# A decoder trunk on one core: start addresses of moving and stationary matmul operands

## Chip, core and metric

The kernel runs on one core of one Trainium2 chip. The metric is the device time of one execution in microseconds: the median of three runs before the change is 1049.02 us (1048.88 to 1049.52).

## What is computed

Two layers over 256 tokens of width 1024, in float32. Each layer is a macaron block: half a SwiGLU feed-forward, a mixer, half a second SwiGLU, and a gated input embedding, each added to the scaled stream and layer-normalised. The mixer is forgetting attention (FoX) in the first layer and multi-head latent attention (MLA) in the second.

```python
def swiglu(x, w_in, w_out):
    h = x @ w_in
    gate, up = h[..., :D_FF], h[..., D_FF:]
    return (jax.nn.silu(gate) * up) @ w_out
...
    for i in range(DEPTH):
        if i == N_A:
            k_nope, k_rope, v_shared = shared_kv(x, kv_w_down, kv_norm, kv_w_up, cos, sin)
        x = post_norm(x, 0.5 * swiglu(x, ffn1_w_in[i], ffn1_w_out[i]), ln_g[i, 0], ln_b[i, 0])
        ...
        x = post_norm(x, mix, ln_g[i, 1], ln_b[i, 1])
        x = post_norm(x, 0.5 * swiglu(x, ffn2_w_in[i], ffn2_w_out[i]), ln_g[i, 2], ln_b[i, 2])
        gate = jax.nn.sigmoid((x @ ple_w_gate[i] + ple_b_gate[i]).astype(jnp.float32)).astype(x.dtype)
        x = post_norm(x, gate * (p[i] @ ple_w_proj[i]), ln_g[i, 3], ln_b[i, 3])
```

D_MODEL is 1024, D_FF 2816, FoX has 16 heads of 64, MLA 16 heads of 128 + 64 (rotary) with a key/value latent of 256 and a query latent of 384.

## The kernel before

Every product is made of three matmuls in TensorE's fast float32 form (`mm3`, L608): each operand is split into a rounded high part and a low remainder, and high·high, high·low and low·high are summed in PSUM. ScalarE writes the high part (`nc.scalar.activation`, L252), VectorE the low part (`tensor_tensor`, L253). `mm(out, lhsT, rhs)` (L615) loads `lhsT` as the **stationary** operand (a LDWEIGHTS of 128 columns, row `PEld` of the profile) and streams `rhs`, the **moving** operand, past it. In a row of the profile, `h<-xT,hl` says that the PSUM bank `h` was written from `xT` and `hl`; it doesn't say which of the two moved.

A stream (`Stream`, L145) brings weights in by DMA in a fixed order, up to three 1 MB groups ahead, and splits them into slots in SBUF: `hl0` to `hl9`, and `gb`, `qk`, `fs`, `ota`, `otb` when these are lent. `place` (L221) makes the tile of a slot: 2112 columns, of which 2048 are used (high part, then low part 4096 bytes further). It starts 48 columns (192 bytes) into the slot for the keys of `moves` (L427): the FoX value weights `fv`, and the gate weights `pg` of layer 0. All other keys start at column 0.

What moves past what, by stage:

- `HT` (L807), most hidden chunks of a feed-forward: weight columns (`wiu`) stationary, the transposed stream `xT` moving, two token tiles of 128 columns in one matmul.
- `H` (L734) through `moving` (L652), two hidden chunks by two token tiles in each of three feed-forwards: `xT` stationary, weights `win` moving, 512 columns.
- `sums` (L859): the hidden activations of a chunk, in seven combinations, stand in one of the four homes `fs`, `qk`, `ota`, `otb` and are stationary; output weights `ws` move, 512 columns. 21 matmuls a chunk.
- FoX: `VA`, `VB`, `VC` (from L1129) with `xT` stationary and `fv` (512 columns), `fvb` (256) and `fvc` (272) moving; the output projection `O` with the attention output in `ota` and `otb` stationary and `fo` moving, 512 columns.
- MLA: `q_rope` with the query latents `cqt` stationary and `qr` moving; `V` with the key/value latents `ckv` stationary and `kvv` moving; `gen` with weights `kvk` and `qn` stationary and `ckv` and `cqt` moving, 256 columns; `QK` with, among others, the rotated queries (in `xT`'s place) stationary and the rotated keys `kr` moving; `O` with the attention output in `otb`, `ota` and `fs` stationary and `mo` moving.
- The input gate `ple` (L1057): `xT` stationary, `pg` moving; 512 columns, and 256 for the last token tile of layer 1.

The order of instructions on each engine is fixed when the program is built: by the lists `FOX` (L49) and `ORDER` (L71) in the mixers, and elsewhere by the stream's own rules, which use estimated times and no addresses. Tiles are laid out in SBUF in the order of their first use. One thing the reader needs beyond the code is where they start; the start address modulo 256 bytes, before:

| tile | start modulo 256 |
|---|---|
| `xT`, `ones` | 160 |
| `fs`, `hl0` to `hl9`, `gb`, `qk`, `g4`, `P` | 224 |
| `ota`, `otb` | 96 |
| `PT` | 160 |
| `ident`, `raw`, `p1` | 128 |

Inside these tiles, operands begin at multiples of 256 bytes from the tile's start, but for the shift of 48 columns, `ckv` (48 columns into `fs`, so 160), and `fvc`, whose blocks of 272 columns begin 1088 bytes apart (64 modulo 256).

Of the kernel before, what the change touches and what calls it, by code (L numbers as in the profile page):

```python
# [10 lines left out]
F32 = mybir.dt.float32  # L11
F32R = mybir.dt.float32r
# [132 lines left out]
class Stream:  # L145
# [74 lines left out]

    def place(self, key, slot):  # L221
        w = self.pool.tile([128, 2112], F32R, tag=slot, name=slot, bufs=1)
        c = 48 if moves(key) else 0
        return w[:, c : c + 2048].rearrange("p (i c) -> p i c", i=2)

    def split(self, half=False):
        self.later()
        nc = self.nc
        key = self.order[self.ready]
        g = group_of(key)  # L230
        while self.sums_left(key):
            self.add(g)
        src, parts, n = unit_of(key, self.raw[g], self.sums.get(g))
        if self.aside(key):
            w = self.pool.tile([128, 2, 512], F32R, tag="g4", name="g4", bufs=6)
        else:
            slot = self.slots.pop(0)
            self.slot_of[key] = slot
            w = self.place(key, slot)
        hi, lo = w[:parts, 0, :n], w[:parts, 1, :n]  # L240
        shape = src.shape
        if len(shape) == 3:
            hi = hi.rearrange("p (a b) -> p a b", b=shape[2])
            lo = lo.rearrange("p (a b) -> p a b", b=shape[2])
        elif len(shape) == 4:
            hi = hi.rearrange("p (a b c) -> p a b c", b=shape[2], c=shape[3])
            lo = lo.rearrange("p (a b c) -> p a b c", b=shape[2], c=shape[3])
        t = self.arrives[group_of(key)]
        self.act_t, self.dve_t = max(self.act_t, t), max(self.dve_t, t)

        def both():
            nc.scalar.activation(hi, src, AF.Copy)  # L252
            nc.vector.tensor_tensor(lo, src, hi.bitcast(F32), op=ALU.subtract)  # L253

        if key[0] == "pb":
            nc.gpsimd.memset(w[:, 0, :].bitcast(F32), 0.0)
            lo = w[32:33, 0, :n]
            both()
        elif half:
            nc.scalar.activation(hi, src, AF.Copy)  # L260
            self.busy(act=n)

            def rest():
                nc.vector.tensor_tensor(lo, src, hi.bitcast(F32), op=ALU.subtract)  # L264
                self.busy(dve=n)
                self.split_done(key, w)

            self.rest = rest
            return
        else:  # L270
            both()
        self.pair(n)
        self.split_done(key, w)

    def aside(self, key):
# [148 lines left out]
    return key  # L424


def moves(key):  # L427
    return key[0] == "fv" or key[:2] == ("pg", 0)


def unit_of(key, raw, sums=None):

    k, u = key[0], key[-1] % 2
    if k in ("win", "fv"):
        return raw.rearrange("p (k c) -> p k c", c=512)[:, 2 * u : 2 * u + 2, :], 128, 1024
    if k == "wiu":
        return raw[:, 1024 * u : 1024 * u + 1024], 128, 1024
    if k == "ws":
        i = key[-1]
        return ((raw, sums)[i // 2])[:, 1024 * u : 1024 * u + (512 if i == 3 else 1024)], 128, 512 if i == 3 else 1024  # L440
    if k == "fvc":
        n = 816 if key[-1] < 2 else 544
        return raw[:, n * u : n * u + n], 128, n
    if k in ("wout", "fvb", "fo", "pg", "pp", "mo", "qr"):
        return raw[:, 1024 * u : 1024 * u + 1024], 128, 1024
    if k in ("fk", "fq"):
        return raw.rearrange("p (k c) -> p k c", c=256)[:, :, 128 * u : 128 * u + 128], 128, 1024
    if k == "pb":
        return raw[0:1, 0:1024], 1, 1024
    if k == "kd":  # L450
        return raw[:, 640 * u : 640 * u + 640], 128, 640
    if k == "dq":
        return raw[:, 768 * u : 768 * u + 768], 128, 768
    if k == "qn":
        return raw[:, 512:1280], 128, 768
    if k == "kvv":
        return raw[:, 0:1024], 128, 1024
    if k == "kvk":
        return raw[:, 0:512], 128, 512
    raise KeyError(key)  # L460
# [50 lines left out]
class Trunk:  # L511
# [24 lines left out]
    def home(self, homes):  # L536

        if self.rec:
            return None, Dummy()
        self.S.retire()  # L540
        tag = next(t for t in homes if t not in self.S.slot_of.values() and t not in self.taken)
        self.taken.add(tag)
        return tag, self.own([128, 2, 896], F32R, tag)

    def dma(self, out, in_):
# [578 lines left out]
    def fox(self, li):  # L1124
        nc, S, a = self.nc, self.S, self.a
# [26 lines left out]
        def VC(t, at={}):  # L1152

            ps = self.bank("y")
            for k in range(8):
                if k in at:
                    at[k]()
                if k % 3 == 0:
                    w = self.use(("fvc", k // 3))
                c = 272 * (k % 3)  # L1160
                self.mm3(
                    ps[:, 0:272], lambda i: self.xT[:, t, i, k, :], lambda i: w[:, i, c : c + 272], k == 0, k == 7)
            if (t, 1) not in v:
                v[t, 1] = self.tl([128, 2, 512], F32R, "g4", 6)
            o = v[t, 1]
            nc.scalar.activation(ftok[:, t, 112:128], ps[:, 256:272], AF.Copy)
            self.parts(o[:, 0, 256:512], o[:, 1, 256:512], ps[:, 0:256])
# [17 lines left out]
        self.tl([128, 8], F32, "gap2", 1)  # L1185
        mb = self.tl([128, 2, 2, 384], F32, "gb", 1)
        cq = self.tl([128, 16, 2], F32, "cq", 1)
        fr = slice(96, 128)
        nc.gpsimd.memset(bf, 0.0)
        if not self.rec:  # L1190
# [3 lines left out]
        f, e, u, r, ab = (fs[fr, 256 * i : 256 * i + 256] for i in range(5))  # L1194
# [224 lines left out]
        def hold(x):  # L1419
# [7 lines left out]
            gb=lambda: self.load_gb(li, 1), ln=lambda t: self.ln(t, y[t], ALPHA, LN_EPS), dl=decay_load, dm=decay_mask,  # L1427
# [47 lines left out]

    def kv_transpose_rope(self):
        nc = self.nc
        self.kr = self.kvt[:, 1088:1856].rearrange("p (i t c) -> p t i c", t=2, i=3)
        kr = [self.kr[:, :, i, :] for i in range(3)]
        b = self.bank("tr")  # L1480
        for t in range(2):
            self.transpose(b[:, 128 * t : 128 * t + 128], self.kvtok[:, t, 256:384])
        nc.gpsimd.memset(kr[1][64:128].bitcast(F32), 0.0)
        nc.gpsimd.memset(kr[2][0:64].bitcast(F32), 0.0)
        b2 = b[:, 0:256].rearrange("p (t c) -> p t c", t=2)
        nc.scalar.activation(kr[0], b2, AF.Copy)
        for s in range(2):
            r = slice(64 * s, 64 * s + 64)
            nc.vector.tensor_tensor(kr[1 + s][r], b2[r], kr[0][r].bitcast(F32), op=ALU.subtract)
# [12 lines left out]
    def mla(self, li):  # L1502
# [3 lines left out]
            self.dma(qn, pbcast(a["mla_q_norm"][0], QR))  # L1506
        scale = float(192 ** -0.5)
        v = {}
        cqt = self.tl([128, 2, 2, 3, 128], F32R, "gb", 1)
        cqtok = self.tl([128, 2, 768], F32, "PT", 1)  # L1510
        S.reclaim("otb", "qk")
        home = {}
# [422 lines left out]
```

## Time and profile before

| | |
|---|---|
| median of three runs | 1049.02 us |
| the profiled execution | 1049.6 us |
| its span | 1047.8 us |
| matmuls | 7085 |
| VectorE busy | 891.8 us |
| ScalarE busy | 592.9 us |
| HBM | 202.74 MB moved by DMA, mean 193 GB/s |

The granted clock is full in all 40 slices of the span. The profile's times are from one execution; all offsets in the rows are counted from its span's start. A matmul's end is modelled and overlaps the next one's start, so of matmuls the starts are to be read, and the distance between them.

### The profile page before, as it was taken

What the parts mean: (1) busy time and instruction counts of PE and PEld (TensorE: products, weight loads), DVE (VectorE), ACT (ScalarE), POOL (GpSimd) and SP (SyncE); (2) the same over time, 40 slices, a digit from 0 to 9 for tenths busy, and PEclk for the clock granted to TensorE, in tenths of its full rate; (3) what the DMA queues carried; (4) which work ended last, traced back from release to release, by engine and by line L of the source; (5) the groups of instructions that cost most, each with busy time, mean ns of one, the idle gap of its engine ahead of it and who ended that gap; (6) DMA issues with size and microseconds to landing.
All of it is one profiled execution on the core that took longest, in us unless ns stands there. A gap on an engine that the chain in (4) does not pass through costs nothing.

```text
span 1047.8 us, 17555 instructions
## 1 busy us (share of the span) xinstructions
PE 1035.6 (99%) x7085; PEld 948.6 (91%) x7085; DVE 891.8 (85%) x1312; ACT 592.9 (57%) x901; POOL 58.0 (6%) x88
## 2 busy tenths in 40 slices
PE   9999999999999999999999999999999999999996
PEld 8999898899889999998899898988999889898986
DVE  5788977868898979978979899888887989889877
ACT  6555563666755555663565646646776564646541
POOL 0000000122300000000220000000000000000000
PEclk9999999999999999999999999999999999999999
DMA  7855586455636363673674545743445564555732
GB/s 281 305 191 188 185 298 243 162 168 169 216 128 246 121 252 125 241 282 132 236 260 151 195 169 190 270 142 112 145 156 179 183 214 162 200 190 176 271 125 81
DMA packets 37476, 202.74 MB, mean 193 GB/s; under 512 B 3970, under 2 KB 9874, under 8 KB 16532
## 3 DMA queue, kind: packets, MB, share of 16 engines
q1 hardware_dynamic: 37396, 201.63, 54.3%
q8 instruction: 55, 0.90, 0.3%
q14 instruction: 25, 0.20, 0.1%
HBM read 200.55 MB, written 1.06 MB: 192 GB/s over the span
## 4 chain that ended last, share of the span: by engine, by line
PE 95%; DVE 2%; ACT 1%; issue 1%; DMA 0%; SPq 0%; DVEq 0%; ACTq 0%
PE h L616 53%; PE y L616 29%; PE tr L616 10%; PE tr L620 2%; DVE hl L253 1%; PE h L620 1%; DMA raw<-in_w_dram 0%; PE tr L1375 0%; DVE ts L300 0%; DVE x L705 0%; DVE tr L1720 0%; ACT qk L629 0%; DVE PT L633 0%; DVE ts L306 0%; DVE raw L308 0%
## 5 line engine op out<-in xcount | busy, mean ns | idle before, releaser
L616 PE MATMUL h<-xT,hl 128*128 128x256 f32 x3144 | 366.1, 277 | 1.2 <-ACT hl L327 0.7
L616 PEld LDWEIGHTS h<-xT,hl 128*128 128x128 f32 x3144 | 362.0, 188 | 2.9 <-ACT hl L327 1.2
L253 DVE TENSOR_TENSOR hl<-raw,hl 128x1024 fp32r<-128x1024 f32 (+5 forms) x271 | 314.2, 1190 | 36.1 <-ACT hl L252 35.0
L252 ACT ACTIVATE hl<-raw 128x1024 fp32r<-128x1024 f32 (+5 forms) x271 | 267.8, 1027 | 70.6 <-DVE raw L308 41.3
L616 PE MATMUL y<-hl,g 128*128 128x512 f32 x336 | 78.6, 391 | 0.0
L616 PEld LDWEIGHTS y<-hl,g 128*128 128x128 f32 x336 | 62.5, 188 | 12.6
L616 PE MATMUL h<-hl,xT 128*128 128x512 f32 (+2 forms) x312 | 67.9, 371 | 0.0
L616 PEld LDWEIGHTS h<-hl,xT 128*128 128x128 f32 x312 | 54.9, 188 | 9.8
L616 PE MATMUL y<-hl,otb 128*128 128x512 f32 x219 | 58.0, 399 | 0.0
L264 DVE TENSOR_TENSOR hl<-raw,hl 128x1024 fp32r<-128x1024 f32 (+2 forms) x44 | 52.3, 1192 | 0.8 <-ACT hl L260 0.7
L616 PE MATMUL y<-hl,xT 128*128 128x512 f32 (+3 forms) x282 | 52.7, 334 | 0.0
L260 ACT ACTIVATE hl<-raw 128x1024 fp32r<-128x1024 f32 (+2 forms) x44 | 45.2, 1029 | 9.7 <-DVE raw L308 9.1
L629 ACT ACTIVATE xT<-tr 128x512 fp32r<-128x512 f32 x28 | 16.1, 597 | 58.9 <-PE tr L620 58.9
L616 PEld LDWEIGHTS y<-hl,xT 128*128 128x128 f32 x282 | 44.1, 188 | 4.6 <-ACT xT L629 0.4
L616 PEld LDWEIGHTS y<-hl,otb 128*128 128x128 f32 x219 | 39.8, 188 | 8.4 <-DVE otb L633 0.3
L616 PE MATMUL y<-hl,ota 128*128 128x512 f32 x177 | 46.8, 398 | 0.1
L700 POOL TENSOR_TENSOR rs<-ve,mhalf 128x1 f32<-128x1 f32 x16 | 15.1, 942 | 519.8 <-DVE ve L699 519.8
L616 PE MATMUL tr<-xT,hl 128*128 128x256 f32 x360 | 42.5, 277 | 0.0
L616 PEld LDWEIGHTS tr<-xT,hl 128*128 128x128 f32 x360 | 41.7, 188 | 0.4
L616 PEld LDWEIGHTS y<-hl,ota 128*128 128x128 f32 x177 | 32.7, 189 | 7.7 <-DVE hl L253 0.6
L823 ACT ACTIVATE P<-h 128x512 f32<-128x512 f32 x33 | 19.7, 596 | 33.0 <-PE h L616 32.6
L300 DVE TENSOR_TENSOR ts<-raw 128x1024 f32<-128x1024 f32 x29 | 35.4, 1222 | 0.6
(322 smaller groups left out, 1632.7 us busy)
## 6 DMA issues: line engine op xcount, KB each, us to landing
raw<-in_ffn_in_dram SPq DMA_DIRECT2D x85, 1024.0 KB, 5.0
raw<-in_ffn_out_dram SPq DMA_DIRECT2D x44, 1024.0 KB, 5.0
raw<-in_pg_dram SPq DMA_DIRECT2D x8, 1024.0 KB, 4.9
raw<-in_mo_dram SPq DMA_DIRECT2D x8, 1024.0 KB, 4.8
raw<-in_kq_dram SPq DMA_DIRECT2D x8, 640.0 KB, 4.2
gb<-in_ln_g_dram SPq DMA_DIRECT2D x8, 512.0 KB, 5.9
gb<-in_ln_b_dram SPq DMA_DIRECT2D x8, 512.0 KB, 7.5
raw<-in_fk_dram SPq DMA_DIRECT2D x4, 1024.0 KB, 5.6
```

The costliest lines, as they stand in the source:

```text
L252: nc.scalar.activation(hi, src, AF.Copy)
L253: nc.vector.tensor_tensor(lo, src, hi.bitcast(F32), op=ALU.subtract)
L260: nc.scalar.activation(hi, src, AF.Copy)
L264: nc.vector.tensor_tensor(lo, src, hi.bitcast(F32), op=ALU.subtract)
L300: tt(s[:, 0:1024].rearrange("p (a b) -> p a b", b=512), r[:, 0:512][:, None, :].to_broadcast([128, 2, 512]), r[:, 512:1536].rearrange("p ( ...
L616: self.nc.tensor.matmul(out, lhsT, rhs, start=start, stop=stop)
L620: self.nc.tensor.transpose(out, in_, self.ident)
L629: self.nc.scalar.activation(hi, src, AF.Copy)
L700: nc.gpsimd.tensor_tensor(rs, ve, self.mhalf, op=ALU.pow)
L823: nc.scalar.activation(gt, ps, AF.Silu)
```

## The change

No instruction is added, removed or moved on any engine, and no DMA changes. Two unused tiles of 128 bytes, `gap4` and `gap5`, are laid out ahead of `ota` and behind the small tiles of FoX: `ota`, `otb` and the statistics tiles behind them begin 128 bytes later than before (`ota` and `otb` so at 224 modulo 256), and all that follows `gap5`, `PT`, `nrm`, `p1` and `raw` among it, 256 bytes later (the same modulo 256). `place` now shifts more keys: by 48 columns (192 bytes) the feed-forward weights `win` that move, `kvv` and `qr`; by 32 columns (128 bytes) `fvb` and `fvc`. The blocks of `fvc` are set 320 columns apart instead of 272, so that their splits write three (or two) pieces of 272 columns instead of one of 816 (or 544). The latents `cqt` lie 192 bytes into their tile, and the rotated keys `kr` 128 bytes further in than before. Modulo 256, moving operands then start as follows:

| moving operand | before | after | stationary operand |
|---|---|---|---|
| `win`, `kvv`, `qr` in `hl`, `qk`, `fs`, `gb` | 224 | 160 | `xT`, `ckv` 160; `cqt` 224, then 160 |
| the same and `fv`, `pg` of layer 0 in `ota`, `otb` | 96, 32 | 160 | 160 |
| `fvb` | 224 | 96 | `xT` 160 |
| `fvc` | 224, 32, 96 | 96 | `xT` 160 |
| `cqt` | 224 | 160 | `qn` 224 |
| `kr` | 224 | 96 | rotated queries 160 |
| `ws`, `fo`, `mo` | 224 | 224 | in `ota`, `otb`: 96, then 224 |
| `xT` | 160 | 160 | weights in `ota`, `otb`: 96, then 224 |

```diff
     def place(self, key, slot):
         w = self.pool.tile([128, 2112], F32R, tag=slot, name=slot, bufs=1)
-        c = 48 if moves(key) else 0
+        c = shift(key)
         return w[:, c : c + 2048].rearrange("p (i c) -> p i c", i=2)
...
         if len(shape) == 3:
-            hi = hi.rearrange("p (a b) -> p a b", b=shape[2])
-            lo = lo.rearrange("p (a b) -> p a b", b=shape[2])
+            b = n // shape[1]
+            hi = hi.rearrange("p (a b) -> p a b", b=b)[:, :, 0 : shape[2]]
+            lo = lo.rearrange("p (a b) -> p a b", b=b)[:, :, 0 : shape[2]]
...
-        self.pair(n)
+        self.pair(math.prod(shape[1:]))
...
-def moves(key):
-    return key[0] == "fv" or key[:2] == ("pg", 0)
+def shift(key):
+
+    if key[0] in ("fv", "kvv", "qr") or key[:2] == ("pg", 0) or key[0] == "win" and key[1:3] != (0, "ffn1"):
+        return 48
+    return {"fvb": 32, "fvc": 32}.get(key[0], 0)
...
     if k == "fvc":
         n = 816 if key[-1] < 2 else 544
-        return raw[:, n * u : n * u + n], 128, n
+        return raw[:, n * u : n * u + n].rearrange("p (a b) -> p a b", b=272), 128, n // 272 * 320
...
         self.taken.add(tag)
+        if tag == "ota":
+            self.tl([128, 32], F32, "gap4", 1)
         return tag, self.own([128, 2, 896], F32R, tag)
...
-                c = 272 * (k % 3)
+                c = 320 * (k % 3)
...
         cq = self.tl([128, 16, 2], F32, "cq", 1)
+        self.tl([128, 32], F32, "gap5", 1)
...
-        self.kr = self.kvt[:, 1088:1856].rearrange("p (i t c) -> p t i c", t=2, i=3)
+        self.kr = self.kvt[:, 1120:1888].rearrange("p (i t c) -> p t i c", t=2, i=3)
...
-        cqt = self.tl([128, 2, 2, 3, 128], F32R, "gb", 1)
+        cqt = self.tl([128, 1584], F32R, "gb", 1)[:, 48:1584].rearrange("p (t i k c) -> p t i k c", t=2, i=2, k=3)
```

## The prediction

> **What bounds the kernel now.** I read the page first, for the engine that sets the end, and then the matmul rows of the timeline, because this change alters nothing but addresses.
>
> ```profile
> PE 1035.6 (99%) x7085; PEld 948.6 (91%) x7085; DVE 891.8 (85%) x1312; ACT 592.9 (57%) x901; POOL 58.0 (6%) x88
> PE 95%; DVE 2%; ACT 1%; issue 1%; DMA 0%; SPq 0%; DVEq 0%; ACTq 0%
> ```
>
> TensorE is busy 99% of the span and carries 95% of the chain that ended last. So a nanosecond off the spacing of matmuls is nearly a nanosecond off the end, unless a wait on another engine takes it back.
>
> The busy time of a row is modelled, so I use the **spacing** instead: the start of the next row minus the start of this one, over the count. Here are three chunks of a `sums` stage, 21 matmuls of 512 columns each (6+3+3+3+3+3), alike but for the home tile of the stationary operand: first `qk`, then `ota`, then `otb`.
>
> ```profile
> 629.26 1.52 PE L616 MATMUL y<-hl,qk 128*128 128x512 f32 x6
> ...
> 634.02 1.56 PE L616 MATMUL y<-hl,ota 128*128 128x512 f32 x6
> ...
> 638.90 1.56 PE L616 MATMUL y<-hl,otb 128*128 128x512 f32 x6
> ...
> 643.78 0.87 PE L616 MATMUL h<-xT,hl 128*128 128x256 f32 x6
> ```
>
> On `qk` the chunk takes 634.02 − 629.26 = 4.76 us, 226.7 ns a matmul. On `ota` and on `otb` it takes 4.88 us, 232.4 ns. By the table of start addresses, the moving operand stands at 224 (modulo 256 bytes) in all three; the stationary one at 224 in `qk` and at 96 in the other two. I call moving minus stationary, modulo 256, the **offset**: 0 against 128. The same operation on the same data sizes costs 5.7 ns more at offset 128.
>
> **The change part by part.** Nothing is removed or added in work: every engine has the same instructions in the same order, and DMAs are the same in size and number. Only three splits of the `fvc` weights write three (or two) separate runs of 272 columns instead of one run. What changes is the offset of some matmuls.
>
> *Sums on `ota` and `otb`, offset 128 to 0.* How many there are comes from these groups:
>
> ```profile
> L616 PE MATMUL y<-hl,otb 128*128 128x512 f32 x219 | 58.0, 399 | 0.0
> L616 PE MATMUL y<-hl,ota 128*128 128x512 f32 x177 | 46.8, 398 | 0.1
> L616 PE MATMUL y<-gb,otb 128*128 128x512 f32 x21 | 5.7, 394 | 0.0
> L616 PE MATMUL y<-gb,ota 128*128 128x512 f32 x3 | 0.9, 393 | 0.0
> L616 PE MATMUL h<-hl,ota 128*128 128x512 f32 x21 | 6.1, 398 | 0.0
> L616 PE MATMUL h<-hl,otb 128*128 128x512 f32 x15 | 4.3, 398 | 0.0
> L616 PE MATMUL h<-gb,otb 128*128 128x512 f32 x3 | 0.9, 398 | 0.0
> ```
>
> A chunk writes `h` three times and `y` twelve times. The `h` rows hold 21 + 15 + 3 = 39, so there are 13 chunks; at 0.12 us each that is 1.56 us. It is not all kept. In one stage VectorE has no slack:
>
> ```profile
> 404.00:440.00 36.00, 36.00 (x232) 32.31 (x231) 35.20 (x43) 22.92 (x27) 0.00 (x0) 1.00 0.51 175
> ```
>
> VectorE is busy 35.20 of 36.00 us there, so TensorE's two chunks in that stage (0.24 us) end in a longer wait for VectorE. I count 11 chunks: **1.32 us**. The bounds are 0 (the offset is not the cause) and 1.56.
>
> *Output projections with the stationary attention output in `ota` or `otb`, offset 128 to 0.* The four `y` rows hold 420 matmuls; without 13 × 12 of the sums, 264 remain. They come in long runs and in sixes:
>
> ```profile
> 286.75 3.11 PE L616 MATMUL y<-hl,otb 128*128 128x512 f32 x12
> 289.70 2.96 PE L616 MATMUL y<-hl,ota 128*128 128x512 f32 x12
> 292.50 2.96 PE L616 MATMUL y<-hl,otb 128*128 128x512 f32 x12
> ...
> 752.06 1.56 PE L616 MATMUL y<-hl,otb 128*128 128x512 f32 x6
> 753.45 1.53 PE L616 MATMUL tr<-hl,fs 128*128 128x512 f32 x6
> ...
> 819.59 4.40 PE L616 MATMUL y<-hl,fs 128*128 128x512 f32 x18
> 823.82 5.75 PE L616 MATMUL y<-hl,ota 128*128 128x512 f32 x24
> 829.40 0.60 PE L620 MATMUL tr<-ident,x 128*128 128x128 f32 x4
> ```
>
> Twelve at offset 128 take 292.50 − 289.70 = 2.80 us, 233.3 ns each; six take 1.39 us, 231.7. The last two heads have their output in `fs` (224, offset 0), and that row speaks for caution: 4.23 us for 18 is 235.0, no better than the 232.5 of the 24 on `ota` behind it. Seen from inside, the run settles:
>
> ```profile
> 822.23 1.76 PE L616 MATMUL y<-hl,fs 128*128 128x512 f32 x7
> ```
>
> The last seven take 823.82 − 822.23 = 1.59 us, 227.1 ns, so the eleven before them took 240 each, start-up included. So offset 0 has to be entered: the first half dozen after a change of work stay slow, and then the spacing locks near 227. For runs of 24 and more (48 in the first mixer, 24 at the end of the second) I take 5 ns on 72: 0.36 us. For the 192 in short runs I take 231.7 − 230 = 1.7 ns, 230 being midway between a settled 227 and the 233.3: 0.33 us. Together **0.7 us**, bounds 0 and 264 × 5.7 ns = 1.5.
>
> *The latents `cqt` moving past `qn` weights, offset 0 to −64, 256 columns.* Here the best offset is another one:
>
> ```profile
> 592.42 24.06 PE L616 MATMUL h<-xT,hl 128*128 128x256 f32 x210
> 616.32 2.88 PE L616 MATMUL h<-xT,gb 128*128 128x256 f32 x24
> ...
> 726.90 1.22 PE L616 MATMUL h<-gb,hl 128*128 128x256 f32 x9
> 727.96 0.49 PE L620 MATMUL tr<-ident,P 128*128 128x128 f32 x3
> ...
> L616 PE MATMUL h<-gb,hl 128*128 128x256 f32 x144 | 19.6, 281 | 0.0
> ```
>
> `xT` (160) past weights at 224, offset −64, takes 23.90 us for 210, 113.8 ns; the latents at offset 0 take 1.06 us for nine, 117.8. Moving them to 160 makes them the first case: 144 × 4.0 ns = **0.58 us**, bounds 0 and 0.65.
>
> *Weights `win` moving past `xT`, offset 64 to 0, 512 columns.* The kernel holds its own comparison. The gate of the per-layer input already shifts its weights in layer 0 and not in layer 1. The same 36 matmuls:
>
> ```profile
> 497.13 2.88 PE L616 MATMUL y<-hl,xT 128*128 128x512 f32 x12
> ...
> 505.34 1.03 PE L620 MATMUL tr<-ident,x 128*128 128x128 f32 x8
> ...
> 1015.85 2.91 PE L616 MATMUL y<-hl,xT 128*128 128x512 f32 x12
> ...
> 1024.11 1.03 PE L620 MATMUL tr<-ident,x 128*128 128x128 f32 x8
> ```
>
> Shifted they take 8.21 us (228.1 ns), unshifted 8.26 (229.4): 1.4 ns. Three feed-forward blocks run four hidden tiles of 24, so 288 × 1.4 ns = **0.4 us**. The upper bound is 288 × (229.4 − 226.7) = 0.8. The lower one is a small loss, since offset 0 is entered slowly. In the second `fv` run, also shifted, 24 take 5.51 us (229.6): 0.1 us lost.
>
> ```profile
> 204.61 1.55 PE L616 MATMUL y<-otb,xT 128*128 128x512 f32 x6
> ...
> 210.12 2.05 PE L616 MATMUL h<-xT,hl 128*128 128x256 f32 x16
> ```
>
> The first six of that run lie in a slot of `otb` and stand at offset 128 even with the shift (`win` there, without it, at −64). There are some 50 such matmuls, weights that landed in `ota` or `otb` and move past `xT`:
>
> ```profile
> L616 PE MATMUL y<-otb,xT 128*128 128x512 f32 x24 | 6.2, 394 | 0.0
> L616 PE MATMUL h<-otb,xT 128*128 128x512 f32 x18 | 4.8, 393 | 0.0
> L616 PE MATMUL h<-ota,xT 128*128 128x512 f32 x12 | 3.4, 401 | 0.0
> ```
>
> All but the second gate's six become like the rest: 48 × 3 ns (an estimate, 232.4 to 229.4), **0.15 us**.
>
> *Weights `fvb` and `fvc` past `xT`, offset 64 (and mixed) to −64, 48 matmuls each.*
>
> ```profile
> 195.48 2.99 PE L616 MATMUL h<-hl,xT 128*128 128x256 f32 x24
> 198.31 3.54 PE L616 MATMUL y<-hl,xT 128*128 128x272 f32 x27
> 201.69 0.60 PE L620 MATMUL tr<-ident,fs 128*128 128x128 f32 x2
> ```
>
> `fvb` takes 2.83 us for 24, 117.9 ns, and goes to the offset at which `xT` runs at 113.8: 0.2 us. `fvc` takes 3.38 us for 27, about 126; with the same 4 ns, 0.2 us, from which I keep half because no run of 272 columns at one offset stands in the trace. **0.3 us**, bounds 0 and 0.4.
>
> *The rest.* `kvv` (48, in sixes) and `kr` (48, in ones and twos) are in runs too short to settle; the `qr` products keep offset 0, as both operands move by 192. I take 0, with ±0.1 us as bounds. Matmuls that read `xT` past weights in `ota` or `otb` go from offset 64 to −64 and stay at the 113.8 of the row above.
>
> The sum is 1.32 + 0.7 + 0.58 + 0.4 + 0.15 + 0.3 = 3.45 us. In the second mixer some of it ends in waits, since scores, softmax and transposes alternate between engines; I take off 0.15. That leaves **3.3 us**. The profiled execution took 1049.6 us (span 1047.8), 0.6 above the median of the runs, and a gain of matmul spacing is the same in each. So the median goes from 1049.0 to **1045.7 us**.
>
> One rule of the notes speaks against all of it. The Trainium skill, "TensorE: Matmul & The Clock Gate", section "Step-by-step: what each phase is for", gives TensorE two independent read ports into SBUF, so that loading the next weights takes nothing from the matmul that runs. By it an offset between the two addresses could not matter and the time would stay 1049.0. The trace differs: 226.7 against 232.4 ns in neighbouring chunks.
>
> **The rivals.** *No price in the address.* The spacing hangs on something that goes with the home tile by chance (its place in the chunk order, say), and all shifts do nothing: 1049.0. For it: `qk` always comes before `ota`. Against it: the gate's 36 matmuls, which differ in layer and shift alone. This is the case that the rule above describes.
>
> *Only long runs gain.* Locking needs ten or more matmuls at one offset. Then sums, latents and the 72 long-run projections count, and the entry of each `win` and `fv` run eats the rest; with waits 1.3 + 0.36 + 0.3 = 2.0 us: 1047.0.
>
> *Everything locks.* Because neighbours now share an offset, runs enter settled: 1.56 + 1.5 + 0.65 + 0.8 + 0.15 + 0.4 = 5.1 us: 1043.9. For it: the chunk on `qk` above entered settled from `fs`.
>
> *The wide majority unlocks (slower).* The 256-column products of `xT` run at 113.8 because they are settled; unsettled, such a product costs the 117.8 of the latents. Weights in `ota` and `otb` reach offset −64 from 64, and a run that enters unsettled could stay so into the rows behind. Each costs 4.0 ns, and the page's largest row has 3144. If all fall it is 12.6 us against 3.3 gained: 1058.3. The point from which the kernel is slower by 0.2% is (3.3 + 2.1) / 4.0 ns, some 1,350 matmuls. Against it: 210 in a row at −64 average 113.8, with transposes just ahead of them.
>
> **How the numbers follow.** Forecast 0.57, everything locks 0.20, only long runs 0.13, no price 0.07, majority unlocks 0.03. The likeliest gives 1045.7. The range runs from 1043.7, just beyond full locking, to 1047.6, just beyond long runs alone. About 0.2% (2.1 us, to 1046.9) is what a measurement of this kernel tells from no change. Faster by more: nearly all of the first two cases and some of the third, 0.79. Within it: 0.18. Slower: 0.03.
>
> **What would show it.** In the changed kernel's timeline, chunks of sums on `ota` and `otb` should take 4.76 us like those on `qk`; the latents' nines about 1.02 us; the first `fvb` run of 24 about 2.73; the long projection run 227 ns once settled; and the wait for VectorE near 429 us should be longer. It is wrong if the `ota` chunks stay at 4.88, or if rows of `xT` past `hl` leave 113.8.

## The result and the profile after

| | before | after |
|---|---|---|
| median in the same rounds (8 runs each) | 1049.27 us (1048.68 to 1050.36) | 1046.36 us (1044.89 to 1048.34) |
| the profiled execution | 1049.6 us | 1046.09 us |
| its span | 1047.8 us | 1044.3 us |

The ratio of the medians is 0.9972, with a 95% interval from 0.9962 to 0.9983: faster by 1.8 to 4.0 us. In five further rounds the same kernel had 1045.69 us beside 1048.97, a ratio of 0.9969 (0.9957 to 0.998).

On the page of the changed kernel the engines' line and the chain of waits read as follows.

```profile
PE 1032.6 (99%) x7085; PEld 948.6 (91%) x7085; DVE 892.0 (85%) x1312; ACT 593.3 (57%) x901; POOL 58.8 (6%) x88
PE 91%; DVE 5%; ACT 1%; issue 1%; DMA 0%; SPq 0%; DVEq 0%; ACTq 0%
```

TensorE still sets the end, and its matmuls are 3.0 us shorter; VectorE's share of the chain has grown from 2 to 5%, since a faster TensorE reaches a few waits sooner. Line 616 is now line 622.

The three chunks of a sums stage, in the timeline of the changed kernel (start, modelled length, engine, line, operands, count); the fourth row begins what follows:

```profile
627.88 1.52 PE L622 MATMUL y<-hl,qk 128*128 128x512 f32 x6
...
632.64 1.52 PE L622 MATMUL y<-hl,ota 128*128 128x512 f32 x6
...
637.40 1.52 PE L622 MATMUL y<-hl,otb 128*128 128x512 f32 x6
...
642.16 0.87 PE L622 MATMUL h<-xT,hl 128*128 128x256 f32 x6
```

4.76 us on each of the three homes, 226.7 ns a matmul. Before, the chunks on `ota` and `otb` took 4.88.

The output projections of the first mixer and the last ones of the second, same view:

```profile
289.48 2.89 PE L622 MATMUL y<-hl,ota 128*128 128x512 f32 x12
292.21 2.88 PE L622 MATMUL y<-hl,otb 128*128 128x512 f32 x12
...
821.55 5.61 PE L622 MATMUL y<-hl,ota 128*128 128x512 f32 x24
826.99 0.60 PE L626 MATMUL tr<-ident,x 128*128 128x128 f32 x4
```

Twelve take 2.73 us (2.80 before), 227.5 ns each; the long run of 24 takes 5.44 (5.58), 226.7 ns each, the settled spacing.

Two groups of nine latents of the second mixer, one of each kind:

```profile
715.74 1.18 PE L622 MATMUL h<-gb,hl 128*128 128x256 f32 x9
716.76 0.84 PE L622 MATMUL h<-fs,hl 128*128 128x256 f32 x6
...
725.04 1.22 PE L622 MATMUL h<-gb,hl 128*128 128x256 f32 x9
726.10 0.49 PE L626 MATMUL tr<-ident,P 128*128 128x128 f32 x3
```

The first nine take 1.02 us (113.3 ns), the second nine 1.06 (117.8), at the same offset of -64. Of the 16 groups 11 are of the first kind and 5 of the second. This pair of spacings comes back in the experiments below.

The first runs of `fvb` (24) and `fvc` (27) in the changed kernel:

```profile
195.45 2.91 PE L622 MATMUL h<-hl,xT 128*128 128x256 f32 x24
198.20 3.48 PE L622 MATMUL y<-hl,xT 128*128 128x272 f32 x27
201.51 0.62 PE L626 MATMUL tr<-ident,fs 128*128 128x128 f32 x2
```

`fvb` went from 2.83 to 2.75 us: from 117.9 to 114.6 ns in this run, of which the last 18 have 113.3; its second run of 24 stayed at 117.8. `fvc` went from 3.38 to 3.31.

The stage near 429 us: its windows row, and the rows around the wait.

```profile
404.00:440.00 36.00, 35.78 (x232) 32.28 (x231) 35.23 (x41) 22.59 (x27) 0.00 (x0) 1.00 0.51 176
```

```profile
427.20 0.87 PE L622 MATMUL h<-xT,hl 128*128 128x256 f32 x6
428.29 0.66 PE L626 MATMUL h<-ident,g 128*128 128x128 f32 x4 [0.22 <-DVE x L890]
```

VectorE is busy 35.23 of the 36.00 us, TensorE now 35.78 instead of 36.00, and the transposes wait 0.22 us for VectorE's `x` where they had not waited.

Where the 3.50 us of span went is read from the matmul rows of both traces: for each of the 7085 the start of the next minus its own start, after minus before, added up by kind.

| kind | matmuls | us |
|---|---|---|
| sums on `ota`, `otb`, outside the stage near 429 us | 231 | -1.25 |
| sums in that stage, and the wait behind them | 42 | -0.23 + 0.24 |
| output projections on `ota`, `otb` | 264 | -0.83 |
| latents past `qn` weights | 144 | -0.41 |
| weights of 512 columns past `xT`, in slots other than `ota` and `otb` | 426 | -0.53 |
| the same in slots of `ota`, `otb` | 54 | -0.18 |
| `fvb`; `fvc` | 48; 48 | -0.08; -0.07 |
| rotated keys `kr` | 48 | +0.11 |
| last gate's quarters, 256 columns, 1024 us on | 95 | -0.40 |
| all of the first 110 us, start-up waits included | | +0.11 |

These make -3.52 us; everything else, waits of the second mixer included, comes to 0.02 us in sum.

The +0.11 hides two large parts: 1.09 us less until 30 us, where the loads' start-up differs from execution to execution, and 1.20 us more from 30 to 110 us. There stand the last 288 products of 256 columns of the first feed-forward; 264 of them in the timeline of the two profiled executions of the changed kernel, the first one first:

```profile
27.60 28.43 PE L622 MATMUL h<-xT,hl 128*128 128x256 f32 x240
55.87 2.99 PE L622 MATMUL h<-xT,gb 128*128 128x256 f32 x24
```

```profile
29.09 27.36 PE L622 MATMUL h<-xT,hl 128*128 128x256 f32 x240
56.29 2.88 PE L622 MATMUL h<-xT,gb 128*128 128x256 f32 x24
```

The same program, the same addresses: the first 240 take 28.27 us (117.8 ns) in one execution and 27.20 (113.3) in the other.

### The profile page after: what moved, and what is told of

Same layout as the page of the kernel before. It is cut to its first block, busy times and chain, and to the rows that moved or that the text cites. A ratio compares the mean times of both kernels' runs of the same rounds, so it can differ in the third digit from the quotient of the medians.

```text
span 1044.3 us, 17555 instructions
## 1 busy us (share of the span) xinstructions
PE 1032.6 (99%) x7085; PEld 948.6 (91%) x7085; DVE 892.0 (85%) x1312; ACT 593.3 (57%) x901; POOL 58.8 (6%) x88
## 3 DMA queue, kind: packets, MB, share of 16 engines
HBM read 200.55 MB, written 1.06 MB: 193 GB/s over the span
## 4 chain that ended last, share of the span: by engine, by line
PE 91%; DVE 5%; ACT 1%; issue 1%; DMA 0%; SPq 0%; DVEq 0%; ACTq 0%
PE h L622 51%; PE y L622 28%; PE tr L622 9%; PE tr L626 2%; DVE hl L254 2%; DVE ts L301 1%; PE h L626 1%; DVE ts L307 0%; DVE raw L309 0%; DMA raw<-in_w_dram 0%; ACT qk L635 0%; ACT hl L253 0%; DVE g L254 0%; PE tr L1382 0%; DVE P L835 0%
```

## The experiments

The theories at the start: **the spacing is set by the offset** (moving minus stationary start, modulo 256 bytes); against it **a locality of the home tile, or of the neighbours in the chunk**. From the runs a third question grew: what chooses between 113.3 and 117.8 ns.

| kernel | median us (range) | before beside it | ratio (95%) |
|---|---|---|---|
| changed kernel, again | 1045.69 (1045.05 to 1047.46) | 1048.97 | 0.9969 (0.9957 to 0.998) |
| unused tiles alone | 1046.94 (1045.38 to 1048.11) | 1049.38 | 0.9973 (0.9962 to 0.9983) |
| shifts alone | 1048.44 (1047.56 to 1049.38) | 1049.38 | 0.9989 (0.998 to 0.9998) |
| without the small offsets | 1045.99 (1044.81 to 1047.19) | 1048.97 | 0.9972 (0.996 to 0.9983) |
| the same again | 1045.70 (1045.04 to 1046.68) | 1049.76 | 0.996 (0.9947 to 0.9972) |
| three narrow products | 1047.21 (1045.53 to 1048.22) | 1049.85 | 0.9971 (0.996 to 0.9981) |
| three narrow products in the flow | 1045.98 (1045.76 to 1046.94) | 1049.76 | 0.9962 (0.9948 to 0.9976) |
| one wide product | 1046.90 (1046.55 to 1048.29) | 1049.85 | 0.9976 (0.9965 to 0.9986) |

### The offset by itself

Nothing but matmuls of fp32r data, in runs of 48, between them four transposes. Behind the first microseconds no other engine works beside them, and DMA moves about 1 GB/s by the profile's page.

```python
def run(out, w, cols, view, m0, s, s0, n):
    cm, cs = (((want - BASE) % 256) // 4 for want in (m0, s0))
    for k in range(n):
        i, j = ((0, 0), (0, 1), (1, 0))[k % 3]
        nc.tensor.matmul(
            out[:, 0:cols], s[:, cs + 256 * i : cs + 256 * i + 128],
            view(w[:, cm + 1152 * j : cm + 1152 * j + 1152]), start=k == 0, stop=k == n - 1)
```

> This kernel computes none of the reference: it only runs matmuls in runs of 48 past a stationary operand, with the moving operand's start 128, 96, 64, 32 or 0 bytes before, or 32, 64 or 96 behind the stationary one's start (modulo 256), for 512, 256 and 272 columns in one piece and for two pieces of 128; once after transposes with the stationary operand at 160 and at 224, once after a run that has settled. Theory (the offset sets the spacing): 512 columns settle at 226.7 ns at offset 0 and at 231 to 233 at -128, whatever the start of the stationary operand; at 64 between, near 229. Two pieces of 128 settle at 113.3 at -64 and 117 to 119 at 0. 256 columns in one piece: 113 at -64 from both entries; at 64 the spacing depends on the entry, 117.7 after transposes and 113.3 after a settled run. Rival (the offset has no price; the kernel's traffic on the other engines makes the difference): all offsets within 0.5 ns of each other. Second rival (the moving start alone counts): the curve for a stationary start of 224 is shifted by 64 bytes against that for 160.

Three runs of 512 columns in its timeline: offset -128 behind transposes, offset 0 behind transposes, offset 0 behind a run that had already settled at 0.

```profile
26.07 11.40 PE L50 MATMUL minus_four<-flat,early 128*128 128x512 f32 x48
37.30 0.60 PE L57 MATMUL minus_three<-ident,x 128*128 128x128 f32 x4
...
72.60 11.16 PE L50 MATMUL zero<-flat,early 128*128 128x512 f32 x48
83.60 0.60 PE L57 MATMUL plus_one<-ident,x 128*128 128x128 f32 x4
...
298.96 11.04 PE L50 MATMUL zero<-flat,early 128*128 128x512 f32 x48
```

The 48 take 11.23, 11.00 and (to 309.84) 10.88 us. Over the last 24 of a run the spacing is 232 to 233 ns at offset -128 and 226.7 at 0; behind transposes the first at 0 takes 0.32 us and the next five some 232 ns each, from a settled run they take 226.7 at once. At 512 columns the values are the same within 1.2 ns for a stationary operand at 160 and at 224, so the offset counts and not where a tile lies. At 512 columns the eight offsets have: 0 226.7; 64 228.9; -64, -32, 32 and 96 233.3; -128 232 to 233; -96 234. At 256 columns: 32 116.7; -96 117.3 to 118.6; -32 118.3; -128, 0 and 96 119 to 120; 64 117.8 here (113.3 is seen in the kernel, below); and -64 either 113.3 or 117.8, constant through a run. So two expectations for 256 columns failed: 113 at -64 from both entries, and 113.3 at 64 behind a settled run. At 272 columns -64 and -96 have 123.3, 64 has 126.7 and 96 has 125.3 to 126.7.

So the rival of the home tile falls, and at 512 columns a price of 5 to 7 ns (offset -128 against 0) is there with nothing beside it.

### The two halves of the change

The first kernel takes the change without its shifts, the second without its unused tiles:

```diff
-        c = shift(key)
+        c = 48 if moves(key) else 0
...
-        cqt = self.tl([128, 1584], F32R, "gb", 1)[:, 48:1584].rearrange("p (t i k c) -> p t i k c", t=2, i=2, k=3)
+        cqt = self.tl([128, 2, 2, 3, 128], F32R, "gb", 1)
```

```diff
-        if tag == "ota":
-            self.tl([128, 32], F32, "gap4", 1)
...
-        self.tl([128, 32], F32, "gap5", 1)
```

In the first, the blocks of `fvc` and the place of `kr` are those of before, too.

> The kernel before with the two unused tiles alone, so that only ota and otb move to 224. Theory: the gain of the sums and projections alone, which the traces before and after put at 2.3 us of matmul starts; less some waits, 2.0 us (0.19%), 1047.3 us beside 1049.3; chunks of sums on ota and otb at 4.76 us, nines of latents still 1.06. Rival (the home's place in the order, not its address, makes it slow): no change, chunks still 4.88. Rival (the gain came from the shifts): under 0.5 us.

> The changed kernel without the two unused tiles: all shifts, but ota and otb back at 96. Theory: what is left is the latents (0.4 us), win (0.4) and the slots in ota and otb (0.2), so 1.0 us (0.1%), 1048.3 us beside 1049.3; together with the gaps it adds up to the whole change. The last 120 matmuls of the gate in layer 1 (offset 64, 256 columns), which the whole change ran at 113.3 instead of 117.7 without touching them, go by how they are entered: they may come out either way. Rival (parts need each other): no gain alone.

The chunks on `ota` and `otb` in the timeline of the unused tiles alone, and then of the shifts alone:

```profile
633.24 1.52 PE L618 MATMUL y<-hl,ota 128*128 128x512 f32 x6
...
638.00 1.52 PE L618 MATMUL y<-hl,otb 128*128 128x512 f32 x6
```

```profile
633.92 1.56 PE L620 MATMUL y<-hl,ota 128*128 128x512 f32 x6
...
638.80 1.56 PE L620 MATMUL y<-hl,otb 128*128 128x512 f32 x6
```

4.76 us with the tiles, 4.88 without. By kind, against before: the tiles alone bring 1.48 us on the sums outside the stage near 429 us, 0.80 on the projections, 0.13 on weights in `ota` and `otb`, and nothing on the latents (+0.04). The shifts alone bring 0.51 on the latents, 0.42 on weights of 512 columns past `xT`, 0.08 on `fvc`, and nothing on the sums (+0.02). In the main each term belongs to the edit that the prediction gave it to; 0.12 us of projections in the shifts alone, and 0.12 us of weights past `xT` in the tiles alone, do not. From 110 us to the end the tiles won 3.10 us and the shifts 1.41, together 0.9 more than the change: 0.23 on the sums (one wait at 114 us, 0.30 us with the tiles alone, 0.53 before and 0.55 after), 0.1 on the latents, a run at 256 us that stood at 113.3 with the shifts alone (0.3), the rest in waits.

The last gate was not foreseen. Its 0.40 us comes with the tiles alone and not with the shifts alone. Nine of its products before and after:

```profile
1029.60 1.22 PE L616 MATMUL y<-hl,xT 128*128 128x256 f32 x9
1030.65 0.28 PE L616 MATMUL y<-hl,ones 128*128 128x256 f32 x1
```

```profile
1026.47 1.18 PE L622 MATMUL y<-hl,xT 128*128 128x256 f32 x9
1027.49 0.28 PE L622 MATMUL y<-hl,ones 128*128 128x256 f32 x1
```

1.05 against 1.02 us, 117 and 113.3 ns, though these weights moved by nothing. What changed is three of the 24 products of each quarter: the weights that lie in `otb` stood at another offset than the rest (-64 among 64), and now stand at 64 with them. All nine profiles of kernels with the unused tiles have it at 113.3, the two without them (before, shifts alone) at 117.6.

### Every fourth byte

> This kernel computes none of the reference: it runs matmuls past a stationary operand at 224. First 36 of 512 columns at each offset from -128 to 124 in steps of 4 bytes, then 36 of two pieces of 128 at the same offsets, then 320 and 384 columns in steps of 32; last, 48 of two pieces of 128 at offset -64, entered after one to eight transposes, and the same with three matmuls of 64 columns, three of 512 columns at offset 0, or six of two pieces at offset 32 between. Theory (the start within 256 bytes counts in steps of 32 or 64): 512 columns at 226.7 ns at 0 and 228.9 at 64, within 1 ns of the neighbour 32 steps' values elsewhere. Two pieces at -64 take one of two spacings, 113.3 or 117.8, and keep it to the end; which one hangs on the entry, so over the eight lengths of transposes both are seen. If one kind of entry always gives 113.3, a run can be set right by it; the rival is that no entry does, and that it is chance (both values in each of the four kinds). Rival to the steps: a smooth curve with its minimum elsewhere, under 226 ns.

The same kind of kernel, with offsets in steps of 4 bytes (36 products each), 320 and 384 columns, and different entries into offset -64. Two neighbours at 512 columns, offsets 0 and 4:

```profile
307.85 8.47 PE L47 MATMUL zero<-flat,late 128*128 128x512 f32 x36
316.16 0.60 PE L55 MATMUL zero<-ident,x 128*128 128x128 f32 x4
316.51 8.75 PE L47 MATMUL zero<-flat,late 128*128 128x512 f32 x36
325.10 0.60 PE L55 MATMUL zero<-ident,x 128*128 128x128 f32 x4
```

8.31 against 8.59 us; settled, 226.7 against 236.7 ns. The 64 offsets lie between 226.7 (at -100, -4, 0, 28, 60 and 108) and 240.0 (at -124, -28 and -12): it is no smooth curve with its best at 0. At 256 columns the least is 113.3 (at 112, settled late) and the most 126.7. At 320 columns every offset has 146.5 to 146.7; at 384 they have 173.3 to 176.7, and the 64 that the kernel uses there is among the best.

Entered in 32 ways (one to eight transposes; behind them nothing, three products of 64 columns, three of 512, or six of 256 at another offset), offset -64 settled at 113.3 in 24 and at 117.8 in 8; each kind of entry had both, and behind the three of 512 columns 7 of 8 were at 113.3. Three and four transposes ahead of the same 48 products:

```profile
1037.37 5.90 PE L47 MATMUL zero<-pair,late 128*128 128x256 f32 x48
...
1043.46 5.70 PE L47 MATMUL zero<-pair,late 128*128 128x256 f32 x48
```

### Without the small offsets

`fvb`, `fvc` and `kr` back where they stood before, the rest as in the changed kernel:

```diff
-    return {"fvb": 32, "fvc": 32}.get(key[0], 0)
+    return 0
...
-        self.kr = self.kvt[:, 1120:1888].rearrange("p (i t c) -> p t i c", t=2, i=3)
+        self.kr = self.kvt[:, 1088:1856].rearrange("p (i t c) -> p t i c", t=2, i=3)
```

> The changed kernel with fvb, fvc and kr as they were before (offset 64, or mixed, and one piece of 816 columns in a split). Theory from the curve (256 columns have two spacings at 64 and at -64 alike, and 272 columns cost 126.7 at 64 and 123.3 at -64): fvb unchanged at 117.9 for the 48; fvc slower by 1 to 2 ns for each of 48; the 32 products with kr faster by about 3 ns each (121.2 back to 117.9). Sum within 0.1 us of the changed kernel, so nothing that a time can show: read from the rows. Rival (the recorded term): 0.3 us slower.

> The changed kernel with fvb, fvc and kr where they stood before. Rows of these three make 0.25 us at the most. Theory (fvb stays at 117.9 ns at offset -64 as at 64, fvc gains 1 to 3 ns on half, kr loses 3 ns on 32; the draw of the first feed-forward decides the rest): the median is within 0.3 us of the changed kernel's for equal draws, so 1045 to 1046.6. Rival (the small shifts cost something by themselves, and the single time of 1045.27 stands for it): 1045.3 with a spread below 1 us.

> The kernel without the small offsets, in the same rounds as the one with kicks: 1045 to 1046.6 if the chip's times are those of the earlier rounds; the time of before beside it says how these rounds stand. Its first 110 us is expected to differ by up to 2.6 us from the other profiles of the same kernel by the draws at 4, 25 and 72 us alone.

`kr` is back at 6.52 us for its 48 (6.63 in the changed kernel, 6.52 before), `fvc` loses the 0.07. From 110 us on, the three profiles of this kernel win 3.62, 4.10 and 4.01 us over before, the two of the changed kernel 3.61 and 3.80; a run of 72 at 256 us that stands at 113.3 or 117.8 makes 0.3 of such a difference. The times, 1045.27, 1045.99 and 1045.70, cannot be told from the changed kernel's 1046.36 and 1045.69. These three edits could have been left out.

### What chooses between 113.3 and 117.8

First the changed kernel once more:

> The changed kernel once more, for its rows: in its first execution the first feed-forward's 480 products of 256 columns ran at 117.8 instead of 113.3 ns from 25 us on (316 of them, 1.4 us), as in the kernel with shifts alone, and not in the kernel before, the one with gaps alone and the one without the small offsets. Theory (this is drawn anew in each execution, where the flow breaks at 25 us for a late weight): it may be fast here, and the span is then 1.4 us shorter, about 1042.9. Rival (it comes with the changed addresses): 313 to 316 slow ones again, span 1044.3. The time over the rounds: 1046.4, from 1044.9 to 1048.3.

Its rows are shown above: the 264 products that ran at 117.8 in the first execution run at 113.3 in this one. But most of the 170 products ahead of 25 us, and a run of 72 at 223 us, ran at 117.8, where the first execution had 113.3, and so the span is again 1044.3 us and not the 1042.9 of the expectation. The state can differ from one execution to the next, though most of it repeats: of the 16 groups of latents 15 have the same state in both executions. In all profiles it holds from a break in the flow of products to the next break. One break stands at the same product in all, product 170 near 25 us: a load of weights waits there, and the spacing is 217 to 226 ns.

Then a kernel of 256-column products at -64 alone, in blocks of 24, with something put between the blocks:

> Computes none of the reference: only matmuls of 256 columns at offset -64 (moving at 160, stationary at 224), which the runs so far showed at 113.3 or at 117.8 ns, in 72 stretches of 4 blocks of 24, a stretch entered by 1 to 4 transposes. Between blocks stands nothing; the three products of a group in another order; one product of 64 columns; one of 512 at offset 0; one transpose; one of 256 columns at offset 32. Theory (the state is set where a run is entered and again where its flow is broken): with nothing between, all four blocks of a stretch keep the state of the first; a disturbance draws it anew, so that slow blocks become fast and fast ones slow, some 6 of 10 fast (20 of 32 entries so far were). Rival (the state hangs on the addresses or on the stretch of time, not on the entry): all blocks of the run are in one state, or change at moments that have nothing to do with the block's edges. A third: a disturbance moves only slow ones to fast, since 113.3 is the stable one; then such a kick is worth 4.5 ns a matmul for all that follow, against 30 to 230 ns for the kick.

The "20 of 32" of this expectation is 24 by the rows above. Nothing between, or another order of the three products: at all 72 edges the state of the block ahead is kept, and of these 24 stretches those entered by one or three transposes are all slow and those by two or four all fast. One product of 64 columns: 36 of 36 blocks behind it at 113.3, three of them from 117.8. One of 512 columns at offset 0: 36 of 36 at 117.8, nine of them from 113.3. One transpose: 24 of 36 at 113.3. One of 256 columns at offset 32: 34 of 36 at 113.3, four of them from 117.8. In the timeline, a stretch that begins slow, with narrow products between:

```profile
293.56 3.07 PE L47 MATMUL minus_two<-pair,late 128*128 128x256 f32 x24
296.47 0.19 PE L58 MATMUL plus_three<-lead,late 128*128 128x64 f32 x1
296.50 2.99 PE L47 MATMUL minus_two<-pair,late 128*128 128x256 f32 x24
299.32 0.19 PE L58 MATMUL plus_three<-lead,late 128*128 128x64 f32 x1
```

From start to start the blocks take 2.91, then 2.82 us (with the entry); a narrow product costs 0.11 to 0.13 us, its slow entry included.

That looked like a handle, so it went into the kernel without the small offsets, ahead of product 192 of the first feed-forward and at two places of the first mixer; and, alone, a wide one ahead of product 192:

```diff
+    def nudge(self, out, w, n=64):
+        self.nc.tensor.matmul(out[:, 0:n], w[:, 0, 0:128], w[:, 0, 0:n], start=True, stop=True)
...
+                        if nudge and (half, k, b) == (0, 0, 0):
+                            self.nudge(ps, w)
```

> The kernel without the small offsets, with three extra products of 64 columns (a weight tile past itself, offset 0) into banks that the next product overwrites: ahead of the second hidden tile of the first feed-forward that both halves of tokens share (product 192 of 480, 28 us), ahead of q of head pair 0 (a run of 72, 212 us) and of k of head pair 6 (a run of 72, 255 us). Everything is computed. Theory (such a product puts the 256-column products behind it at 113.3 ns, as in 36 of 36 blocks alone): the 288 behind the first run at 113.3 whatever came ahead; the run at 212 us falls from 8.66 to 8.3 us, the kick included, in every execution; the one at 255 us takes 8.2 to 8.3 where it took 8.48 or 8.16. About 113 ns for each kick: 0.2 us won at 212, 0.1 to 0.2 at 255 on the mean, and at 28 us 1.3 in the executions that ran slow there (2 of 8 profiles) less 0.1 in each: a median near 1045.4 against 1046.0, and fewer executions above 1047. Rival (in the kernel the traffic of the other engines and of the DMA decides the state): the three runs stay in the states that the profiles of before had, 117.8 at 212, and the kernel loses 0.3 us.

> The kernel without the small offsets, with one extra product of 512 columns at offset 0 at product 192 of the first feed-forward (28 us), into a bank that the next product overwrites. Everything is computed. Theory (such a product puts the 256-column products behind it at 117.8 ns, as in 36 of 36 blocks alone): the 288 behind it run at 117.8, 1.3 us, and the product itself takes 0.24: 1.5 us slower than the kernel without it, 1047.5, in nearly every execution. Rival (the state is drawn): slow in some 3 of 10 executions as without it, and 0.24 us slower on the median, 1046.2.

The rows around product 192, narrow and then wide:

```profile
27.73 1.07 PE L622 MATMUL tr<-xT,hl 128*128 128x256 f32 x8
28.63 0.19 PE L626 MATMUL h<-hl 128*128 128x64 f32 x1
28.66 27.45 PE L622 MATMUL h<-xT,hl 128*128 128x256 f32 x240
55.95 2.88 PE L622 MATMUL h<-xT,gb 128*128 128x256 f32 x24
```

```profile
26.83 1.46 PE L622 MATMUL tr<-xT,hl 128*128 128x256 f32 x11
28.12 0.39 PE L626 MATMUL h<-hl 128*128 128x512 f32 x1
28.35 28.43 PE L622 MATMUL h<-xT,hl 128*128 128x256 f32 x240
56.62 2.99 PE L622 MATMUL h<-xT,gb 128*128 128x256 f32 x24
```

The 240 take 27.29 us behind the narrow product and 28.27 behind the wide one, as the theory had it. But the rows just ahead say that neither product set this: the eight ahead of the narrow one already take 0.90 us (113 ns each), the eleven ahead of the wide one 1.29 (117). In both executions the state had changed some 20 products earlier, at the break near 25 us: at product 170 from 117.8 to 113.3 with the narrow product, and from 113.3 to 117.8 with the wide one. In the first mixer, behind other work, the narrow products changed nothing: 8.66 us for the 72 at 214 us (8.66 without), 8.56 at 257 (8.48 or 8.16 without). And the run of 282 at 72 us, which no edit touched, took 33.30 us in the execution with the narrow products, as it did with the unused tiles alone, where most have 32.06. The median came out at 1047.21, beside a kernel before whose median of 1049.85 was 0.5 to 0.9 above that of the earlier rounds.

Last, the narrow products only between products of the same kind:

> The kernel without the small offsets, with three extra products of 64 columns, each now between two runs of 256-column products and not behind transposes: at product 192 of the first feed-forward (28 us), ahead of the second half of the hidden tile at 72 us (product 42 of 282) and ahead of k of head pair 1 (product 24 of the 72 at 212 us). Everything is computed. Theory (a narrow product sets the state where it stands between products of the same kind, as alone and at 28 us in the last run; behind transposes the state is drawn again): the 48 products behind the third kick run at 113.3 although the 24 ahead run at 117.8, so 0.22 us less 0.11; the 240 behind the second are at 113.3 whatever came ahead; the 288 behind the first too. Rival (the run at 212 us is held at 117.8 by what runs beside it there): its 48 stay at 117.8 and the three kicks cost 0.3 us. The median by the theory: 0.1 to 0.5 us below the same kernel without kicks in the same rounds.

```profile
26.81 1.22 PE L622 MATMUL tr<-xT,hl 128*128 128x256 f32 x9
27.87 0.20 PE L626 MATMUL h<-hl 128*128 128x64 f32 x1
27.90 28.51 PE L622 MATMUL h<-xT,hl 128*128 128x256 f32 x240
56.25 2.99 PE L622 MATMUL h<-xT,gb 128*128 128x256 f32 x24
```

28.35 us for the 240: at the same place, with the same product, they now run at 117.8, as the nine ahead did (1.06 us). At 216 us the 48 behind the third narrow product stay at 117.8; at 77 us the 240 behind the second run at 113.3, as those ahead did. The theory that a narrow product sets the state falls for this kernel: at all four places between products of the same kind it left the state as it stood just ahead, and so did the wide one at its place. The wide one is not shown to set it either, as the products ahead of it were slow already. Its median of 1046.90 does not tell, since 1047.5 was expected if the state were always slow, 1046.2 if drawn. The median of the last kernel, 1045.98 us, is 0.3 above that of the same kernel without the products (1045.70), not 0.1 to 0.5 below. What decides the state at a break stays open. Products alone repeat their pattern from stretch to stretch, so it is not noise; what the kernel has besides is DMA and the other engines writing to the memory that TensorE reads. That was not tried apart.

No version here is shown to beat the changed kernel.

## Why the prediction was right

The forecast was 3.3 us of spacing and a median of 1045.7, in a range from 1043.7 to 1047.6. From 110 us to the end the rows gave 3.61 us; the median was 1046.36. Step by step:

- **TensorE sets the end, so spacing is time.** Held: the start of the last matmuls moved by what the spacings add up to, 3.5 us.
- **Sums, 1.32.** 1.25 by the rows. The two chunks near 429 us gained 0.23 and the wait behind them grew by 0.24, as the full VectorE there had said.
- **Output projections, 0.7.** 0.83. Short runs enter slowly, as assumed; settled runs of 24 have 226.7.
- **Latents, 0.58.** 0.41. The mechanism held and the size was off: 113.8 was taken as the price of the offset, and a settled 113.3 is one of two prices of the same offset. Five groups of nine drew 117.8.
- **Weights past `xT`, 0.4, and slots, 0.15.** 0.53 and 0.18.
- **`fvb` and `fvc`, 0.3.** This step failed: 0.15. It read 113.8 from a run with `xT` moving and gave it to weights moving at the same offset. Both offsets turn out to have both prices. At -64 the first run of `fvb` settled at 113.3 and the second at 117.8, in each of the three profiles that have it there; at 64 the first stays at 117.8, and the second had 113.3 in four of eight profiles. `fvc` gained 0.07. (Its 3.38 us for 27 are 125.2 ns each, and not about 126.)
- **The rest, 0.** `kr` lost 0.11, just outside the 0.1 allowed.
- **Waits of the second mixer, -0.15.** Waits grew by 0.18 and 0.15 us near 255 and 771 us and shrank elsewhere; in sum nothing is left of this term.
- **Not in the sum:** the last gate, 0.40 us won, because three of 24 products no longer stand at another offset than their neighbours. The prediction had set that gate aside as unchanged; that runs which share an offset enter settled was a reason of the rival "everything locks", and here it decided.

That a gain of spacing is the same in each execution, as the step from the profile to the median had it, does not hold. The difference between 3.6 us of rows and 2.9 of medians is within the interval of the ratio, and the changes of state are large enough for it: the 264 products above are worth 1.2 us, the 282 at 72 us as much, and the eight times of the changed kernel spread over 3.45 us.

Of the rivals, "no price in the address" falls with the products alone. There the Trainium skill's two independent read ports ("TensorE: Matmul & The Clock Gate", section "Step-by-step: what each phase is for"), by which the offset cannot matter, differ from the measurement: 226.7 and 233 ns with nothing else running. What the load and the matmul share was not shown. But the traces say which load it is: before the change, the last product on `qk`, itself at offset 0, takes 232 to 233 ns to the next start in all seven places where sums on `ota` follow (226 to 227 after the change). The last on `otb`, itself at offset 128, takes 226 to 227 in all six places where weights at 224 follow; the one such place behind `ota`, near 119 us, has 231. So the time to the next start goes, in the main, with the weights that are loaded for the next product. "Only long runs gain" falls with the sums, all in threes, whose chunks enter settled. "The majority unlocks" named a real mechanism, with 4.5 ns instead of the 4.0 and for one run at a time. Its sign, that rows of `xT` past `hl` leave 113.8, was seen: the 240 above ran at 117.8 in the first execution of the changed kernel, and at 113.3 in the second. That the change makes it more frequent is not shown, since the kernel before has one profile.

## What to carry to other kernels

When TensorE is the bound and two groups of equal matmuls differ by 2 to 5%, compare the start addresses of their operands, and price an offset by matmuls alone before moving tiles: 48 products for each offset, their second half read, were enough here at 512 columns; at 256 enter each offset more than once. Move the operands so that all matmuls in a stage share one good offset, since in the last gate here three strangers among 24 cost all of them the settled spacing (117.6 against 113.3 ns). Read one profile's spacing as one sample: where a run has two spacings at the same addresses, profile the kernel more than once before giving the difference to an edit.

## What the runs showed of the hardware

- At equal addresses and with nothing beside it, a run of 256-column fp32r products at offset -64 has 113.3 or 117.8 ns (in the kernel at 64 as well), and keeps it until its flow is broken.
- Four bytes between two starts change the spacing of 512-column products from 226.7 to 236.7 ns; at 320 columns no offset of eight changes anything (146.5 to 146.7).
- With matmuls alone, one product of 512 columns at offset 0 left 36 of 36 blocks behind it in the slower state (three of them behind transposes only 1 of 8), one of 64 columns 36 of 36 in the faster one; in the kernel both left the state as it stood just ahead, at all five places between products of 256 columns.
- The first 512-column products of an execution took 426 to 427 ns each in place of 226.7: 11 of them behind a first one of 594 ns in one of the two offset kernels, 6 behind a first one of 592 in the other.
- In the kernel before, the time from one 512-column product to the next went with the offset between its moving operand and the weights of the next product: 232 to 233 ns for a product at offset 0 ahead of weights at offset 128 (7 of 7 places), 226 to 227 the other way round (6 of 7).
